# First norm, first v groups, late output projection and the samples' scores of a streaming encoder: the order of work changed

## The chip, the core and the metric

The kernel runs on one core of a Trainium2 chip. The metric is the device time of one execution in microseconds (us): the median of the runs before the change is 3111.28 us (three runs, 3106.77 to 3111.31). Engines are called PE (TensorE; its weight loads appear as PEld), DVE (VectorE), ACT (ScalarE), POOL (GpSimd) and SP (SyncE, which issues most DMAs). Two of PE's clock levels appear in the granted clock of the profile: 2.4 GHz, shown as 1.0, and 1.2 GHz, shown as 0.5.

## What is computed

One step of a 4-layer encoder with 512 tokens of a new stream (the prompt) and 8 running streams with 16 tokens each (the samples), 640 tokens in all, model width 1024:

```
for layer in range(4):                       # kinds A, B, C, A
    hp, hs = rms_norm(xp), rms_norm(xs)
    A: differential attention; prompt chunk-causal, samples over 1024 cached + 16 own positions
    B: Griffin recurrent block
    C: band attention with relative bias; samples over 512 cached + 16 own positions
    x = x + mixer(h) ;  x = x + square(relu(rms_norm(x) @ w1)) @ w2
y = rms_norm(x)

A, a sample:  p = softmax(q @ [k_cache; k_own]^T * 64**-0.5)   per head, for two half heads
              o = (p_1 - lam * p_2) @ [v_cache; v_own] ;  o = rms_norm(o) @ w_out
```

New keys and values of the attention layers and the states of layer B are outputs too.

## The kernel before, in words

**Layout.** The residual lies transposed on chip: 8 tiles `x[d]` of 128 features by 640 tokens. A matrix product in full precision is made of three matmuls with a high and a low part of each operand: high with high, low weights with high data, high weights with low data (L566 to L568 for projections to q, k and v with 256 columns; L473 to L475 with 320 columns elsewhere). ACT makes the high part (`wh` of weights, L223; `xh`, L331), DVE the low part (`wl`, L224; `xl`, L332).

**Order.** The kernel is written as loops; a scheduler then sets the order of each engine's instructions by the order in which they are emitted, a priority, and what it takes each to last. PE has eight PSUM banks under four tags: "mm" (2), "s" (2), "t" (3), "o" (1).

**First norm.** `Normed` with `first=True` makes `xh`, `xl` and squares of the eight input tiles. Squares alternate between DVE (L347) and ACT (L349); POOL adds six of them to `sacc` (L350) and DVE the last. Five matmuls with a column of ones sum over features (L375); POOL then takes the power -0.5 (L379, `rtok`), by which ACT and DVE scale the first v tiles when they leave PSUM (L581, L582).

**First v groups.** `v_group(0, tt)` for the five token tiles calls `x_group`, 24 matmuls into one bank each (tags mm, s, mm, s, t).

**Attention layers.** Eight slots (two heads of C or one head of A each); in each slot four prompt units and two sample units (q = 0, 1, four streams each) go through stages f0 to f4, and between them the projections of the next slot run. A sample unit's f0 (L785 on) makes the scores over the cache: per bank of 512 positions (two in A, one in C) four matmuls of 32 output rows side by side in the PE array (`tile_position`, L796), one for each stream. The unit's own 16 positions are four matmuls of 32 rows and 16 columns (L800) into a "t" bank. DVE takes the maximum of each piece (L816 in A, with the bias in L819 in C), ACT the exponential (L823), and POOL spreads the own block's 16 columns over a 128 x 128 tile with a 0/1 mask (L825, `eox`). f1 transposes (L838, L845), f2 multiplies with the values (L856 for the own block, L860 for the cache, 32 rows side by side again), f3 combines the halves (L877, `os` to `oc`), scales by the norm (L665 on DVE, L667 and L668 on POOL), f4 transposes `oc` (L892). For a prompt unit the same stages are L683/L684, L717, L730 (C: L741) and L751.

**Output projection.** In the last slot's steps (`s == SLOTS`) nothing is left to project, and the loop emits 21 pieces evenly over ten steps instead: one transpose, four splits (L963, L964) and 16 `early` groups, 12 matmuls each, which are the part of the output projection over the first four heads. Behind the loop come the rest of the splits and the late part.

**End.** The last MLP's output adds to `x` (L1203), ACT squares (L1210), POOL and at j = 7 DVE sum the squares (L1211), a ones matmul (L1216), the power (L1219), a broadcast (L1221), and the product to `y` (L1224), for each of the two halves of the tokens.

Of the kernel before, what the change touches and what calls it, by code (L numbers as in the profile page):

```python
# [135 lines left out]
def hybrid_encoder_kernel(ctx: ExitStack, tc: tile.TileContext, I, O):  # L136
# [165 lines left out]
    halves = load_const("halves", [P, 2])  # L302
    ropec = load_const("ropec", [P, 2, TT, 32])
# [13 lines left out]
    class Normed:  # L317
# [19 lines left out]
        def square(self, d):  # L337
            n = self.n
            self.n += 1
            if self.first:  # L340
# [4 lines left out]
                sq = self.work.tile([P, N], F32, tag="sq", name="sq", bufs=4)  # L345
# [162 lines left out]
    def attention(layer, kind, xg, aw, op):  # L508
# [50 lines left out]
        def x_group(w, tt, tag="mm"):  # L559
            acc = bank(tag)  # L560
            (h0, l0), (h1, l1) = w
            ts = slice(tt * P, (tt + 1) * P)
            for k in range(KT8):
# [7 lines left out]
        wcur = {}  # L571

        def v_group(p, tt):
# [5 lines left out]
            acc = x_group(wcur["v"], tt, ("mm", "s", "mm", "s", "t")[tt] if p == 0 else "mm")  # L579
# [202 lines left out]
        class Sample:  # L782
# [3 lines left out]
            def f0(self):  # L786
# [4 lines left out]
                sc = [bank("s") for _ in range(npc)]  # L791
                ow = bank("t")
                for c in range(npc):
                    for j in range(4):
                        b = 4 * q + j
                        pe.matmul(sc[c][32 * j:32 * j + 32, :], lhsT=z[:, b].rearrange("p a q -> p (a q)"),  # L796
                                  rhs=KV["k", s, b][:, c * 512:(c + 1) * 512], start=True, stop=True, tile_position=(0, 32 * j))
                for j in range(4):
                    b = 4 * q + j
                    pe.matmul(ow[32 * j:32 * j + 32, :16], lhsT=z[:, b].rearrange("p a q -> p (a q)"),  # L800
                              rhs=KTt[s][:, 16 * b:16 * b + 16], start=True, stop=True, tile_position=(0, 32 * j))
# [4 lines left out]
                src = [t[:, :] for t in sc] + [ow[:, :16]]  # L806
# [4 lines left out]
                eo = aw.tile([P, 16], F32, tag="eo", name="eo", bufs=2)  # L811
                self.E.append(eo)
                m = npc + 1
                for c, t in enumerate(src):
                    if is_a:
# [6 lines left out]
                for c, t in enumerate(src):  # L822
                    act.activation(self.E[c], t if is_a else self.E[c], AF.Exp, bias=st[:, 4:5], accum_out=st[:, 5 + c:6 + c])  # L823
# [587 lines left out]
    for d in range(KT8):  # L1411
        cur.add(d)
        if d >= 2:
            cur.square(d - 2)
# [196 lines left out]
```

## Time and profile before

| | us |
|---|---|
| median of three runs | 3111.28 |
| the profiled execution's own time | 3111.17 |
| its span, first to last instruction | 3109.4 |
| PE busy | 3040.6 (98%) |
| DVE busy | 2431.5 (78%) |
| ACT busy | 1619.0 (52%) |
| POOL busy | 509.7 (16%) |

The profiled execution took 0.1 us less than the median. PE is without work for some 69 us of the span. The rows are read so: a start in us from the span's first instruction, a duration, the engine, the line of the kernel, the operation, output <- input, and how many were merged (xN). In brackets behind a row stands the time that the engine was idle ahead of it and what it waited for. One fp32 matmul of the samples or of a 128 x 128 product shows as two records, a transposition as one. Matmuls overlap, so what one costs PE is the distance from its start to the next start, not its duration.

### The profile page before, as it was taken

The page shows a single profiled execution, that of the slowest core. Times are in us where ns is not written, and L with a number is a line of the kernel's source. Part 1 is how long each engine was busy: PE and PEld are TensorE (multiplying, and loading weights), DVE is VectorE, ACT ScalarE, POOL GpSimd, SP SyncE. Part 2 cuts the span into 40 slices and gives each one's busy share as a digit, 9 for nine tenths or more (in the row PEclk, how much of TensorE's full clock was granted, in tenths as well). Part 3 has the DMA queues.
Part 4 walks back from the last instruction along what each step waited for, and adds up shares of the span by engine and source line. Part 5 has one row for each costly group of instructions (what it writes and reads, how often), then busy time and mean ns, then how long its engine had stood idle before and what let it go on. Part 6 is the DMA issues. An engine that isn't in the chain of part 4 may idle for free. (4 is left out here: it accounts for less than half of the span.)

```text
span 3109.4 us, 61475 instructions
## 1 busy us (share of the span) xinstructions
PE 3040.6 (98%) x23970; PEld 2896.8 (93%) x23970; DVE 2431.5 (78%) x5197; ACT 1619.0 (52%) x3180; POOL 509.7 (16%) x676
## 2 busy tenths in 40 slices
PE   8999999999999999999999999999999999999998
PEld 7888799999999999999988889999998887999998
DVE  7777788887788788788566679788867776888877
ACT  4666554444477544445566655444446665544443
POOL 5443200000044000000222200000044432000001
PEclk9999999999999999999999999999999999999999
DMA  6877622222312322223666532222268776222223
GB/s 232 275 260 274 229 72 82 82 82 82 107 62 70 86 82 79 79 88 108 196 200 200 171 112 69 82 82 88 90 188 282 263 263 226 76 82 82 82 82 102
DMA packets 169682, 423.49 MB, mean 136 GB/s; under 512 B 19248, under 2 KB 49968, under 8 KB 169392
## 3 DMA queue, kind: packets, MB, share of 16 engines
q1 hardware_dynamic: 144336, 394.51, 37.9%
q0 software_dynamic: 4032, 9.18, 1.7%
q10 hardware_dynamic: 21024, 15.89, 1.6%
q8 instruction: 189, 3.10, 0.4%
q14 instruction: 101, 0.83, 0.1%
HBM read 379.24 MB, written 18.50 MB: 128 GB/s over the span
## 5 line engine op out<-in xcount | busy, mean ns | idle before, releaser
L223 ACT ACTIVATE wh<-raw 128x1024 fp32r<-128x1024 f32 (+1 forms) x396 | 368.8, 932 | 369.4 <-PE ps_t L1004 103.1
L224 DVE TENSOR_TENSOR wl<-raw,wh 128x1024 fp32r<-128x1024 f32 (+1 forms) x396 | 431.3, 1090 | 80.6 <-ACT wh L223 77.6
L566 PE MATMUL ps_mm<-wh,xh 128*128 128x256 f32 x1344 | 388.7, 290 | 8.4 <-ACT wh L223 8.3
L568 PE MATMUL ps_mm<-wh,xl 128*128 128x256 f32 x1344 | 387.8, 289 | 4.4 <-DVE xl L332 4.4
L567 PE MATMUL ps_mm<-wl,xh 128*128 128x256 f32 x1344 | 386.4, 288 | 0.1
L223 ACT ACTIVATE wh<-wsum 128x1024 fp32r<-128x1024 f32 x184 | 193.9, 1056 | 189.4 <-PE ps_o L1004 42.5
L566 PEld LDWEIGHTS ps_mm<-wh,xh 128*128 128x128 f32 x1344 | 256.7, 191 | 22.4 <-ACT wh L223 8.3
L568 PEld LDWEIGHTS ps_mm<-wh,xl 128*128 128x128 f32 x1344 | 256.4, 191 | 21.4 <-issue 14.8
L567 PEld LDWEIGHTS ps_mm<-wl,xh 128*128 128x128 f32 x1344 | 256.9, 191 | 8.5 <-issue 5.8
L361 POOL DMA_DIRECT2D sacc<-sq x28 | 24.9, 888 | 1295.3 <-ACT sq L359 1240.7
L224 DVE TENSOR_TENSOR wl<-wsum,wh 128x1024 fp32r<-128x1024 f32 x184 | 223.8, 1218 | 12.3 <-ACT wh L223 12.1
L1045 ACT ACTIVATE v<-v 128x640 f32<-128x640 f32 x128 | 93.2, 731 | 168.7 <-DVE v L1095 146.5
L607 POOL TENSOR_TENSOR rs<-ss,negh 128x4 f32<-128x4 f32 x120 | 130.2, 1085 | 227.0 <-DVE ss L605 182.8
L475 PE MATMUL ps_s<-hh,wl 128*128 128x320 f32 x512 | 158.3, 309 | 0.0
L475 PE MATMUL ps_mm<-hh,wl 128*128 128x320 f32 x512 | 158.2, 309 | 0.0
L474 PE MATMUL ps_mm<-hl,wh 128*128 128x320 f32 x512 | 158.2, 309 | 0.0
L473 PE MATMUL ps_mm<-hh,wh 128*128 128x320 f32 x512 | 158.2, 309 | 0.0
L473 PE MATMUL ps_s<-hh,wh 128*128 128x320 f32 x512 | 158.1, 309 | 0.0
L474 PE MATMUL ps_s<-hl,wh 128*128 128x320 f32 x512 | 158.0, 309 | 0.0
L1005 PE MATMUL ps_t<-fbh,wl 128*128 128x320 f32 x448 | 139.0, 310 | 0.0
L1003 PE MATMUL ps_t<-fbh,wh 128*128 128x320 f32 x448 | 138.8, 310 | 0.0
L1004 PE MATMUL ps_t<-fbl,wh 128*128 128x320 f32 x448 | 138.7, 310 | 0.0
(478 smaller groups left out, 10166.0 us busy)
## 6 DMA issues: line engine op xcount, KB each, us to landing
raw<-in_w SPq DMA_DIRECT2D x260, 512.0 KB, 4.1
kk<-in_cak SPq DMA_DIRECT2D x128, 512.0 KB, 6.7
vv<-in_cav SPq DMA_DIRECT2D x128, 512.0 KB, 5.8
raw<-in_wax SPq DMA_DIRECT2D x48, 512.0 KB, 4.7
kk<-in_cck SPq DMA_DIRECT2D x32, 512.0 KB, 4.6
vv<-in_ccv SPq DMA_DIRECT2D x32, 512.0 KB, 4.5
raw<-in_wcx SPq DMA_DIRECT2D x24, 512.0 KB, 4.5
sacc<-sq POOLq DMA_DIRECT2D x28, 320.0 KB, 4.6
```

The source lines that it names most:

```text
L223: act.activation(dst, src, AF.Copy)
L224: dve.tensor_sub(low, src, dst.bitcast(F32))
L473: pe.matmul(acc[:, :HALF], lhsT=wh[:, cs], rhs=a, start=k == 0, stop=False)
L474: pe.matmul(acc[:, :HALF], lhsT=wh[:, cs], rhs=b, start=False, stop=False)
L475: pe.matmul(acc[:, :HALF], lhsT=wl[:, cs], rhs=a, start=False, stop=k == ks - 1)
L566: pe.matmul(acc[:, :256], lhsT=xg.hi[k][:, ts], rhs=wh[:, cs], start=k == 0, stop=False)
L567: pe.matmul(acc[:, :256], lhsT=xg.hi[k][:, ts], rhs=wl[:, cs], start=False, stop=False)
L568: pe.matmul(acc[:, :256], lhsT=xg.lo[k][:, ts], rhs=wh[:, cs], start=False, stop=k == KT8 - 1)
L607: pool.tensor_tensor(rs, ss, negh[:, :4], op=ALU.pow)
L1003: pe.matmul(acc, lhsT=wh[:, cs], rhs=a, start=start and k == 0, stop=False, skip_group_check=True)
L1004: pe.matmul(acc, lhsT=wh[:, cs], rhs=b, start=False, stop=False, skip_group_check=True)
L1005: pe.matmul(acc, lhsT=wl[:, cs], rhs=a, start=False, stop=k == 3, skip_group_check=True)
```

## The change

Five edits, together:

- **First norm and first v groups.** All squares go to ACT, all sums to DVE; the loops first emit every `xh`/`xl` and then the squares. The five banks of the first v groups are filled feature tile by feature tile (k outermost) instead of bank after bank.
- **Own block.** The mask becomes additive (0 and -1e30). The own block is one full 128 x 128 product of four streams' queries with all 128 own keys (L810 of the changed kernel, for L800), whose other 7/8 the mask takes out; the maximum and the exponential run over 128 columns and write `eox` directly. L825 on POOL goes. In C POOL adds bias and mask into one 128 x 128 tile ahead of the maximum, and the own block's bank carries the tag "s" instead of "t".
- **Scores in one piece.** The matmuls of a unit's cache scores have a priority higher by 400 and an order among themselves (`add_manual_dep`); the two banks are taken in reverse order.
- **Late output projection.** In the last slot the 16 early groups are emitted four each in the last four steps.
- **End.** DVE sums the squares from j = 5 on.

```diff
+    dve.tensor_scalar(own, own, 1e30, -1e30, op0=ALU.mult, op1=ALU.add)
...
-                if n % 2:
-                    dve.tensor_mul(sq, x[d], x[d])
-                else:
-                    act.activation(sq, x[d], AF.Square)
-                (dve if n == KT8 - 1 else pool).tensor_add(self.acc, self.acc, sq)
+                sq = self.work.tile([P, N], F32, tag="sq", name="sq", bufs=KT8 - 1)
+                act.activation(sq, x[d], AF.Square)
+                dve.tensor_add(self.acc, self.acc, sq)
...
+                FIRST.extend(bank(t) for t in ("mm", "s", "mm", "s", "t"))
+                for k in range(KT8):
+                    for i in range(TT):
+                        x_group(wcur["v"], i, acc=FIRST[i], ks=(k,))
...
-                for j in range(4):
-                    b = 4 * q + j
-                    pe.matmul(ow[32 * j:32 * j + 32, :16], lhsT=z[:, b].rearrange("p a q -> p (a q)"),
-                              rhs=KTt[s][:, 16 * b:16 * b + 16], start=True, stop=True, tile_position=(0, 32 * j))
+                sc = [bank("s") for _ in range(npc)][::-1]
+                ow = bank("t") if is_a else bank("s")
+                with tc.high_priority(offset=400):
...
+                    for a, b in zip(g[1:], g):
+                        tc.add_manual_dep(a.ins, b.ins.name, IN_ORDER, reason="one piece")
+                pe.matmul(ow[:, :P], lhsT=z[:, 4 * q:4 * q + 4].rearrange("p b a q -> p (b a q)"), rhs=KTt[s], start=True, stop=True)
...
-                pool.tensor_mul(self.eox, eo[:, None, :].to_broadcast([P, 8, 16]),
-                                own[:, q].rearrange("p (b t) -> p b t", t=16))
+                for c in range(m):
+                    e = self.E[c] if c < npc else self.eox
+                    act.activation(e, sc[c] if is_a and c < npc else e, AF.Exp, bias=st[:, 4:5], accum_out=st[:, 5 + c:6 + c])
...
+            if s == SLOTS:
+                n = len(g) - 2 * KT8
+                tgt = [min(n, 3 * k) for k in range(nst + 1)] + [n + 4 * k for k in range(1, 5)]
...
-                    (dve if j == KT8 - 1 else pool).tensor_add(acc2, acc2, sq)
+                    (dve if j >= KT8 - 3 else pool).tensor_add(acc2, acc2, sq)
...
-        if d >= 2:
-            cur.square(d - 2)
-    cur.square(KT8 - 2)
-    cur.square(KT8 - 1)
+    for d in range(KT8):
+        cur.square(d)
```

How the change moves instructions is shown at three places. The first is DVE at the start of the program, while the x tiles are split; `sq` are squares, `sacc` their sum. Before:

```order
4 L347 TENSOR_TENSOR sq<-x_79 128x640
5 L224 TENSOR_TENSOR wl<-raw,wh 128x1024
6 L332 SCALAR_TENSOR_TENSOR xl<-x_79,gains,xh 128x640
7 L347 TENSOR_TENSOR sq<-x_83 128x640
8 L332 SCALAR_TENSOR_TENSOR xl<-x_81,gains,xh 128x640
9 L332 SCALAR_TENSOR_TENSOR xl<-x_83,gains,xh 128x640
```

After:

```order
3 L224 TENSOR_TENSOR wl<-raw,wh 128x1024 x2
4 L334 SCALAR_TENSOR_TENSOR xl<-x_79,gains,xh 128x640
5 L349 TENSOR_TENSOR sacc<-sacc,sq 128x640
6 L334 SCALAR_TENSOR_TENSOR xl<-x_81,gains,xh 128x640
7 L349 TENSOR_TENSOR sacc<-sacc,sq 128x640 x2
8 L334 SCALAR_TENSOR_TENSOR xl<-x_83,gains,xh 128x640
```

The squares have left DVE, the sums have come to it, and POOL has no row in this stretch any more. The second place is PE in the first layer, where the scores of one unit (eight matmuls `kk,qs`) and its own block (`kt,qs`) stand between projections. Before:

```order
830 L730 MATMUL ps_o<-v,et 128x128
831 L796 MATMUL ps_s<-kk,qs_235 32x512 x7
832 L717 MATMUL ps_t<-ident,e 128x128
833 L796 MATMUL ps_s<-kk,qs_235 32x512
834 L566 MATMUL ps_mm<-wh,xh 128x256
...
842 L800 MATMUL ps_t<-kt,qs_235 32x16 x4
```

After:

```order
L805 MATMUL ps_s<-kk,qs_236 32x512 x8
L889 MATMUL ps_t<-os,jq 128x128 x2
L567 MATMUL ps_mm<-wl,xh 128x256
L568 MATMUL ps_mm<-wh,xl 128x256
L566 MATMUL ps_mm<-wh,xh 128x256
L567 MATMUL ps_mm<-wl,xh 128x256
L723 MATMUL ps_t<-ident,e 128x128
L810 MATMUL ps_t<-kt,qs_236 128x128
```

The eighth score matmul stands with the other seven, and one full product stands for four tiled ones. The third place is PE at the end of the first layer's attention: the last unit's values, its halves (`os,jq`), the last transpositions and the late output projection (`oh,wh`). Before:

```order
2049 L860 MATMUL ps_o<-vv,et 32x128 x32
2050 L717 MATMUL ps_t<-ident,e 128x128 x4
2051 L751 MATMUL ps_t<-ident,oc 128x128
2052 L877 MATMUL ps_t<-os,jq 128x128
2053 L473 MATMUL ps_mm<-oh,wh 128x320
...
2065 L877 MATMUL ps_t<-os,jq 128x128
2066 L730 MATMUL ps_o<-v,et 128x128 x4
2067 L892 MATMUL ps_t<-ident,oc 128x128
2068 L751 MATMUL ps_t<-ident,oc 128x128
2069 L473 MATMUL ps_mm<-oh,wh 128x320
```

After:

```order
2070 L872 MATMUL ps_o<-vv,et 32x128 x32
2071 L723 MATMUL ps_t<-ident,e 128x128 x4
2072 L757 MATMUL ps_t<-ident,oc 128x128
2073 L889 MATMUL ps_t<-os,jq 128x128 x2
2074 L736 MATMUL ps_o<-v,et 128x128 x4
2075 L904 MATMUL ps_t<-ident,oc 128x128
2076 L757 MATMUL ps_t<-ident,oc 128x128
2077 L472 MATMUL ps_mm<-oh,wh 128x320
```

The twelve early matmuls (rows 2053 to 2064 of before) have left the tail for places further up, and both halves of the last unit's outputs stand together.

## Rows read from the trace of the kernel before

**Rows 1.** Page, first part: busy time, share and instructions of PE.
```profile
PE 3040.6 (98%) x23970; PEld 2896.8 (93%) x23970; DVE 2431.5 (78%) x5197; ACT 1619.0 (52%) x3180; POOL 509.7 (16%) x676
```

**Rows 2.** Busy time by stretch (us from:to, length, engines, clock, DMA share, GB/s).
```profile
60.00:300.00 240.00, 238.89 (x2531) 209.00 (x2530) 182.46 (x614) 150.28 (x468) 98.40 (x128) 1.00 0.78 269
386.60:393.50 6.90, 4.58 (x16) 4.00 (x16) 3.43 (x5) 3.54 (x6) 1.50 (x3) 0.51 0.22 76
```

**Rows 3.** Waits of PE, 0 to 60 us (us in total, times, longest).
```profile
PE ps_mm L566 <- ACT wh L223: 8.3, 1, 8.3
PE ps_mm L568 <- DVE xl L332: 4.4, 3, 2.5
```

**Rows 4.** Timelines of DVE, POOL and ACT at the start, and one DVE line over all.
```profile
11.81 2.19 DVE L332 SCALAR_TENSOR_TENSOR xl<-x,gains,xh 128x640 fp32r<-128x640 f32 x1
23.91 3.74 DVE L332 SCALAR_TENSOR_TENSOR xl<-x,gains,xh 128x640 fp32r<-128x640 f32 x3
10.90 4.49 POOL L350 TENSOR_TENSOR sacc<-sacc,sq 128x640 f32<-128x640 f32 x2 [10.02 <-ACT xh L331]
16.07 2.25 ACT L331 ACTIVATE xh<-x,gains 128x640 fp32r<-128x640 f32 x3
L332 DVE SCALAR_TENSOR_TENSOR xl<-x,gains,xh x32: 871/884/2187, 5.3 to 2274.6; 128x640 fp32r<-128x640 f32 x32
```

**Rows 5.** Timeline of PE around one sample unit of layer 0.
```profile
63.81 0.28 PE L567 MATMUL ps_mm<-wl,xh 128*128 128x256 f32 x1
64.02 1.92 PE L796 MATMUL ps_s<-kk,qs 128*32 128x512 f32 x16
65.88 0.39 PE L568 MATMUL ps_mm<-wh,xl 128*128 128x256 f32 x1
66.10 0.28 PE L566 MATMUL ps_mm<-wh,xh 128*128 128x256 f32 x1
66.22 0.28 PE L567 MATMUL ps_mm<-wl,xh 128*128 128x256 f32 x1
...
67.01 0.26 PE L800 MATMUL ps_t<-kt,qs 128*32 128x16 f32 x8
67.20 0.39 PE L566 MATMUL ps_mm<-wh,xh 128*128 128x256 f32 x1
...
69.81 0.38 PE L730 MATMUL ps_o<-v,et 128*128 128x128 f32 x2
...
70.15 0.28 PE L567 MATMUL ps_mm<-wl,xh 128*128 128x256 f32 x1
```

**Rows 6.** Timeline of PE where a unit's scores are broken, layer 0.
```profile
146.29 1.92 PE L796 MATMUL ps_s<-kk,qs 128*32 128x512 f32 x14
...
148.40 1.05 PE L796 MATMUL ps_s<-kk,qs 128*32 128x512 f32 x2
149.37 0.39 PE L566 MATMUL ps_mm<-wh,xh 128*128 128x256 f32 x1
```

**Rows 7.** What the score matmuls of L796 waited for, all layers (us, times).
```profile
  ACT e L690: 4.1, 6
```

**Rows 8.** Timelines at the ends of attention in layers 0 and 2: PE, then DVE.
```profile
381.49 0.39 PE L473 MATMUL ps_mm<-oh,wh 128*128 128x320 f32 x1
...
383.33 0.38 PE L877 MATMUL ps_t<-os,jq 128*128 128x128 f32 x2
...
387.58 0.47 PE L892 MATMUL ps_t<-ident,oc 128*128 128x128 f32 x1 [2.97 <-POOL oc L668]
389.87 0.64 PE L473 MATMUL ps_mm<-oh,wh 128*128 128x320 f32 x1 [1.24 <-ACT oh L963]
...
1823.11 0.49 PE L877 MATMUL ps_t<-os,jq 128*128 128x128 f32 x2 [1.23 <-DVE os L868]
...
384.47 1.22 DVE L224 TENSOR_TENSOR wl<-raw,wh 128x1024 fp32r<-128x1024 f32 x1 [0.25 <-ACT wh L223]
```

**Rows 9.** Timeline of DVE at the end of the program.
```profile
3098.34 0.49 DVE L1211 TENSOR_TENSOR fsum<-fsum,fsq 128x320 f32<-128x320 f32 x1 [1.40 <-POOL fsum L1211]
```

More of the change, by code (lines that the diff above doesn't have):

```diff
@@ L302, in hybrid_encoder_kernel @@
     halves = load_const("halves", [P, 2])
+    dve.tensor_scalar(own, own, 1e30, -1e30, op0=ALU.mult, op1=ALU.add)
+    IN_ORDER = mybir.DependencyInfo(mybir.DependencyClass.NoSync, mybir.DependencyReason.DATA)
     ropec = load_const("ropec", [P, 2, TT, 32])
@@ L557, in load_bias, with x_group @@
             SB[s] = sb
-        def x_group(w, tt, tag="mm"):
-            acc = bank(tag)
+        def x_group(w, tt, tag="mm", acc=None, ks=range(KT8)):
+            if acc is None:
+                acc = bank(tag)
             (h0, l0), (h1, l1) = w
             ts = slice(tt * P, (tt + 1) * P)
-            for k in range(KT8):
+            for k in ks:
                 wh, wl = (h0, l0) if k < 4 else (h1, l1)
@@ L569, in x_group @@
             return acc
-        wcur = {}
+        wcur, FIRST = {}, []
         def v_group(p, tt):
@@ L790, in f0 @@
                 st = aw.tile([P, 12], F32, tag="sst", name="sst", bufs=3)
-                sc = [bank("s") for _ in range(npc)]
-                ow = bank("t")
-                for c in range(npc):
-                    for j in range(4):
-                        b = 4 * q + j
[L796 to L799, printed above, removed]
-                    pe.matmul(ow[32 * j:32 * j + 32, :16], lhsT=z[:, b].rearrange("p a q -> p (a q)"),
-                              rhs=KTt[s][:, 16 * b:16 * b + 16], start=True, stop=True, tile_position=(0, 32 * j))
+                sc = [bank("s") for _ in range(npc)][::-1]
+                ow = bank("t") if is_a else bank("s")
+                with tc.high_priority(offset=400):
+                    g = []
+                    for c in range(npc):
+                        for j in range(4):
+                            b = 4 * q + j
+                            g.append(pe.matmul(sc[c][32 * j:32 * j + 32, :], lhsT=z[:, b].rearrange("p a q -> p (a q)"),
+                                               rhs=KV["k", s, b][:, c * 512:(c + 1) * 512], start=True, stop=True,
+                                               tile_position=(0, 32 * j)))
+                    for a, b in zip(g[1:], g):
+                        tc.add_manual_dep(a.ins, b.ins.name, IN_ORDER, reason="one piece")
+                pe.matmul(ow[:, :P], lhsT=z[:, 4 * q:4 * q + 4].rearrange("p b a q -> p (b a q)"), rhs=KTt[s], start=True, stop=True)
                 if q == 0:
@@ L805, in f0 @@
                     load_k(s + 1, 0)
-                src = [t[:, :] for t in sc] + [ow[:, :16]]
                 self.E = []
@@ L837, in f1 @@
                 t = bank("t")
-                pe.transpose(t[:, :P], self.eox.rearrange("p a b -> p (a b)"), ident)
+                pe.transpose(t[:, :P], self.eox, ident)
                 et = aw.tile([P, P], F32, tag="eto", name="eto", bufs=2)
```

26 lines of the change are left out of this document (14 added, 12 removed).

## The prediction

> **What bounds the kernel now.** I read the page's busy times first: PE works 3040.6 of 3109.4 us [rows 1], so PE sets the time, and it can only be shortened in two ways: less work on PE, or fewer of the 69 us in which it stands. Then the busy time by stretch: between 60 and 300 us, the heart of the first attention layer, PE is busy 238.89 of 240 us, while DVE has 182.46 and the DMA engines 0.78 of the stretch [rows 2]. So inside an attention layer a microsecond that PE does not work is a microsecond won, as long as DVE (24% free there) and the loads follow. Then PE's waits at the start: 8.3 us for the first weights, which the change does not touch, and 4.4 us in three waits for the low parts of x [rows 3]. Then the timeline of PE around a sample unit [rows 5, 6], which shows what a tiled matmul costs those around it; and last the ends of the attention layers and of the program [rows 8, 9], where PE stands for a chain over ACT, DVE and POOL. The MLPs and layer B keep their order, so these hold the same time.
>
> **First norm and first v groups.** The low part of one x tile takes DVE 0.884 us in the median and 2.187 at worst; the 2.19 at 11.81 lies beside POOL's two sums from 10.90 to 15.39 [rows 4]. All long ones lie beside POOL sums. With POOL out of this stretch, DVE has eight low parts and seven sums of about 0.8 us. ACT gets three or four more squares, some 0.7 each, like its high parts (2.25 for three [rows 4]). ACT's last high part, now ready at 18.3, comes with the squares ahead of it at about 21 (18.3 + 3.5 x 0.75); DVE, whose fifteen steps follow ACT's, has three or four of 0.8 left by then and makes the last low part at about 24, against 27.65 now (23.91 + 3.74 [rows 4]). The k-outermost order gives PE 115 matmuls that need no later tile, so PE should run without a stop from 8.3. The three waits are 4.4 us in all [rows 3]. I count 3.7 for the two long ones in full, and 1.1 for the short one with the small stops around it, room for nine matmuls of 0.12: **-4.8 us**. The rest of the chain (sum, power, v out of PSUM, first keys) moves with it. Bounds: if the loads or the DVE chain keep the longest wait of 2.5 us [rows 3], -2.3; at best -5.5, all waits and the small stops twice. One mask instruction more on DVE lies under the loads.
>
> **Own block and scores: the price of a tiled run.** In the timeline plain matmuls of 256 columns stand 0.12 apart (66.10 to 66.22). Ahead of eight score matmuls the distance is 0.21 (63.81 to 64.02), and the first plain matmul behind them takes 0.22 (65.88 to 66.10) [rows 5]. So a run of tiled matmuls costs 0.09 on the way in and 0.10 on the way out, 0.19 beside what is in it. In it: eight score matmuls 1.86 (64.02 to 65.88); four own-block matmuls 0.19 (67.01 to 67.20) [rows 5]. Scores that were broken seven and one cost 2.11 for the seven with the transposition behind them (146.29 to 148.40), no less than eight with what follows (2.08), and 0.97 more for the one (148.40 to 149.37) [rows 6]: one matmul alone costs half of what eight cost, since four lie side by side. A whole 128 x 128 product in fp32 costs 0.22 (two records of L730 and the next matmul from 69.81 to 70.15, less 0.12) [rows 5].
>
> Counting runs in the order of instructions: 160 before (55, 46 and 59 in the three attention layers), 110 after (43, 24, 43). Of 48 own blocks 37 stood alone and 11 behind scores, where I take 0.05, a quarter of 0.19, since the way in and out is paid already. Eight units had their scores broken in uneven pieces, after it one. Six more value runs are cut in halves. The sum:
> - 50 runs fewer x 0.19 = -9.5
> - seven broken pieces fewer x 0.97 = -6.8
> - tiled own blocks gone: 37 x 0.19 + 11 x 0.05 = -7.5
> - whole own blocks added: 48 x 0.22 = +10.6
> - cut value runs: no row shows one; by the switch of 0.19 they are counted above, and I add 6 x 0.15 = +0.9 inside them.
>
> Together **-12.3 us**, some -2.5 in layer 0, -6 in C, -4 in layer 3. Bounds: a switch that is partly a wait for the weights, and so not given back, leaves -12.3 + 9.5 = -2.8; the most, if a whole product cost only one of L730's two records, 0.11, is -17.6. What the change adds elsewhere lies beside PE: the maximum and the exponential over 128 columns instead of 16 on DVE and ACT (48 times, at most some 0.1 us each), for which POOL's spreading goes out of the chain exponential, mask, transposition.
>
> The Trainium skill, page "TensorEngine Tiling (Array Packing)", section "When to Use Tiling", speaks against this part: for at most 32 rows or columns it recommends four tiles side by side, which is what goes. By that rule the own block gets slower; inside a run the rows agree (0.19 against 0.22), and only the switch, which the same page names under "Key Properties" as a drain, turns it.
>
> **Late output projection.** At the end of layer 0's attention PE goes from 381.49, where the last values and transpositions are done, to the late projection at 389.87: 8.38 us, of which twelve early matmuls take 1.84 (to 383.33) and two waits 2.97 and 1.24 [rows 8]. The chain that fills it is: halves combined, copy on DVE, behind it a weight split on DVE of 1.22 us ahead of the norm's scale, POOL's power and scaling, transposition, two splits. After the change no early matmul stands in it; they are done earlier, in place of nothing, since PE is full there too. Both halves come together, and the weight split goes ahead of the copy instead of between copy and scale. From the same point I estimate 0.4 us to the combined halves, 0.3 copy, 0.45 norm, 1.5 for the scale and POOL, 2.3 from the transposition to the late projection (387.58 to 389.87): some 5.0, with 0.2 for what lies between, 5.2, against 8.38 - 1.84 = 6.54. That is -1.35 in each of layers 0 and 3 (the tail of layer 3 reads alike). In C ten early matmuls now stand where PE waits 1.23 us for the copy `os` [rows 8]: -1.2. Sum **-3.9 us**. PE's granted clock is 0.51 from 386.6 to 393.5 [rows 2], behind the wait; I leave that as it is. Bounds: +2, if the halves wait uncovered and the weight split still delays the copy (1.22 a layer [rows 8], less what was won); -7.5, if with a shorter wait the clock stays up, which gives back half of the 3.6 us from 389.87 to 393.5 in both A layers.
>
> **End.** The last sum starts at 3098.34 after 1.40 us in which DVE waited for POOL's sum [rows 9]. With DVE doing the last three sums only ACT's square of the last x, about as long as the sum's 0.49, lies between: 1.40 - 0.5 and a little, **-0.8 us**; bounds 0 and -1.2.
>
> **Sum:** -4.8 - 12.3 - 3.9 - 0.8 = -21.8 us, on the profiled execution's own 3111.17: 3089.4. That execution stands 0.1 us from the median, so I say 3089.5.
>
> **Rivals.**
> - *The switch is not given back* (other matmuls carry its wait, the weights' load or the bank it writes): part two gives -2.8 and the whole is 3111.2 - 12.3 = 3099. For it: the same 0.09 could be a stop that the next foreign kind of matmul, the whole fp32 product, meets as well (the 256-column matmul behind L730 starts its follower 0.21 later, too, which is inside my 0.22). Against it: 0.22 counted both.
> - *The whole own block is the slower one.* Its switch does not come back, since it stands beside other foreign kinds of matmul, while whole scores and merged runs gain as forecast: 37 x 0.19 = 7.0 less, 3089.4 + 7.0 = 3096.4. For it: 0.22 against 0.19 inside [rows 5]. Against it: in the same rows the matmul behind the tiled block pays. This is the result that the Trainium skill's page "TensorEngine Tiling (Array Packing)" would lead to.
> - *Slower: PSUM banks.* Scores with a raised priority take both "s" banks as soon as they can, and in C the own block wants one of them too. PE runs in order: if the bank is still read by a prompt unit's exponential, all projections behind stand. Before, the score matmuls waited 4.1 us in six waits for that exponential (L690) [rows 7], 0.7 each. If each of the 48 units waits as long once, that is 33 us: 3089.4 + 33 = 3122, slower. It decides from 0.45 us a unit. Against it: the banks' readers stand in the same distances in the order as before.
> - *The change does not do what it says*: the tails lose cover (+2 for -3.9) and only half of the start comes: 3089.4 + 5.9 + 2.5 = 3098.
>
> **How the numbers follow.** Forecast as summed, within the bounds of its parts: 0.62, 3076 to 3096. Whole own block the slower one: 0.08, about 3096. Switch not given back: 0.09; tails and start short: 0.08; both 3096 to 3105. Nothing that can be told, from parts that cancel: 0.07. Slower by the banks: 0.06, 3118 to 3140. About 0.2% (6 us) is what a measurement of this kernel can tell from no change; 3105 is that border. The range 3077 to 3104 leaves out the best end of the first case, the last two cases and the rim of the second. Faster by over 0.2%: 0.62 + 0.08 + 0.09 + 0.08 less 0.02 = 0.85; within: 0.07 + 0.02 = 0.09; slower: 0.06.
>
> **What would show it.** Start: PE without a wait between 8.3 and the ones matmul, no POOL sum, low parts at 0.88 us; the ones matmul (now L374) about 5 us earlier. Scores: eight matmuls in one row of the timeline, 0.22 around the own block, PE's busy time some 10 us shorter with about 50 switches fewer. Tails: the wait ahead of the transposition of `oc` (L904) shorter than 2.97. End: DVE's last sum within 1 us of the last x. It is wrong if PE's waits on ACT's or DVE's readers of "s" banks grow past 10 us, if PE's idle share in 60 to 300 us rises above 1%, or if the stretch from the first matmul of a layer to its last does not shrink by the sums above.

## The result and the profile after

The changed kernel takes 3091.94 us in the median of four runs (3090.58 to 3092.30); the kernel before took 3111.30 beside it. The ratio is 0.9938, with a 95% interval of 0.9924 to 0.9953: 19.4 us less. The forecast was 3089.5 with a range of 3077 to 3104. The total came out; two of its four terms did not. That the total came so close is in part luck.

The page of the changed kernel, first part, answers to [rows 1]:

```profile
span 3090.1 us, 60938 instructions
PE 3025.0 (98%) x23682; PEld 2898.4 (94%) x23682; DVE 2432.5 (79%) x5236; ACT 1624.6 (53%) x3184; POOL 477.0 (15%) x634
```

The span is 19.3 us shorter. PE's busy time fell by 15.6 us (from 3040.6), and what it stood idle fell from 68.8 to 65.1 us, by 3.7. So the gain is mostly less work on PE.

**Start.** PE's waits in the first 60 us of the changed kernel (answer to [rows 3]; us in total, times, longest):

```profile
PE ps_mm L566 <- ACT wh L223: 9.2, 1, 9.2
PE ps_mm L568 <- DVE xl L334: 0.5, 1, 0.5
```

Its DVE timeline there (answer to [rows 4]), the first low part behind the first weights and the last one:

```profile
11.59 0.88 DVE L334 SCALAR_TENSOR_TENSOR xl<-x,gains,xh 128x640 fp32r<-128x640 f32 x1
23.14 0.88 DVE L334 SCALAR_TENSOR_TENSOR xl<-x,gains,xh 128x640 fp32r<-128x640 f32 x1
```

All eight low parts take 0.88 us now, the last is ready at 24.02 (23.14 + 0.88), and 0.5 us of the 4.4 us of waits are left. In the kernel before, the three long low parts (2.15 to 2.19 us) each ended 0.7 us after the end of a sum on POOL that had begun ahead of them. PE's timeline has the ones matmul at

```profile
24.07 1.17 PE L374 MATMUL ps_t<-ones,sacc 128*128 128x1 f32 x10
```

and that of before at

```profile
29.64 1.28 PE L375 MATMUL ps_t<-ones,sacc 128*128 128x1 f32 x10
```

It moved by 5.6 us, by 6.4 if counted from each run's first matmul, since the first weights came 0.9 us later in this run (9.2 against 8.3). That arrival lies between 7.5 and 9.2 us in the traces of all kernels of this study.

**A sample unit of layer 0**, PE's timeline of the changed kernel (answer to [rows 5]):

```profile
59.83 1.92 PE L805 MATMUL ps_s<-kk,qs 128*32 128x512 f32 x16
61.68 0.39 PE L566 MATMUL ps_mm<-wh,xh 128*128 128x256 f32 x1
61.91 0.28 PE L567 MATMUL ps_mm<-wl,xh 128*128 128x256 f32 x1
62.02 0.28 PE L568 MATMUL ps_mm<-wh,xl 128*128 128x256 f32 x1
62.14 0.27 PE L723 MATMUL ps_t<-ident,e 128*128 128x128 f32 x1
62.25 0.39 PE L810 MATMUL ps_t<-kt,qs 128*128 128x128 f32 x2
62.39 0.36 PE L566 MATMUL ps_mm<-wh,xh 128*128 128x256 f32 x1
62.59 0.28 PE L567 MATMUL ps_mm<-wl,xh 128*128 128x256 f32 x1
```

Eight scores stand together. The own block costs 0.22 us: from 62.25 to 62.59 are 0.34, less 0.12 for the plain matmul in it.

**Ends of the layers**, PE's timeline at the end of layer 0's attention (answer to [rows 8]):

```profile
381.47 0.33 PE L904 MATMUL ps_t<-ident,oc 128*128 128x128 f32 x1 [1.17 <-POOL oc L674]
382.87 0.33 PE L757 MATMUL ps_t<-ident,oc 128*128 128x128 f32 x1 [1.08 <-POOL oc L674]
384.42 0.63 PE L472 MATMUL ps_mm<-oh,wh 128*128 128x320 f32 x1 [1.22 <-ACT oh L978]
```

One wait of 2.97 us became two of 1.17 and 1.08.

**By stretches.** From the starts of the first projection and of the first late projection matmul in each layer, and the first matmul of the program:

| stretch | before | after | change | forecast |
|---|---|---|---|---|
| first weights on PE | 8.31 | 9.17 | +0.9 | 0 |
| first matmul to layer 0's late projection | 381.56 | 375.25 | -6.3 | -4.8 - 2.5 - 1.35 = -8.65 |
| attention of layer 2 | 351.40 | 341.62 | -9.8 | -6 - 1.2 = -7.2 |
| from there to layer 3's first projection | 446.20 | 447.91 | +1.7 | 0 |
| attention of layer 3 | 373.05 | 367.03 | -6.0 | -4 - 1.35 = -5.35 |
| all else (MLPs, layer B, end) | | | +0.2 | -0.8 |

Each column is one execution. The kernel before and the kernel of experiment e3 have the same instructions in the same order on every engine, and yet layer 0's stretch takes 381.56 us in one and 383.62 in the other, layer 3's 373.05 and 371.99. The changed kernel and that of e9 have the same order up to the last MLP's end, and layer 2's attention takes 341.62 and 339.50. So a stretch that changes by less than some 2 us says nothing by itself.

PE's timeline at the two ends of layer 2's attention, of the kernel before:

```profile
1474.63 0.28 PE L566 MATMUL ps_mm<-wh,xh 128*128 128x256 f32 x1
...
1826.03 0.41 PE L473 MATMUL ps_mm<-oh,wh 128*128 128x320 f32 x1 [1.15 <-ACT oh L966]
```

and of the changed kernel:

```profile
1468.68 0.28 PE L566 MATMUL ps_mm<-wh,xh 128*128 128x256 f32 x1
...
1810.30 0.41 PE L472 MATMUL ps_mm<-oh,wh 128*128 128x320 f32 x1 [1.15 <-ACT oh L981]
```

### The profile page after: what moved, and what is told of

The parts are those of the page before. It is cut to its first block, busy times and chain, and to the rows that moved or that the text cites. A ratio compares the mean times of both kernels' runs of the same rounds, so it can differ in the third digit from the quotient of the medians.

```text
span 3090.1 us, 60938 instructions
## 1 busy us (share of the span) xinstructions
PE 3025.0 (98%) x23682; PEld 2898.4 (94%) x23682; DVE 2432.5 (79%) x5236; ACT 1624.6 (53%) x3184; POOL 477.0 (15%) x634
## 4 chain that ended last, share of the span: by engine, by line
PE 78%; DVE 5%; issue 2%; ACT 2%; DMA 1%; POOL 1%; SPq 0%; ACTq 0%; DVEq 0%; POOLq 0%
PE ps_t L1018 5%; PE ps_t L1020 5%; PE ps_t L1019 5%; PE ps_mm L472 4%; PE ps_mm L473 4%; PE ps_mm L474 4%; PE ps_s L472 3%; PE ps_s L473 3%; PE ps_s L474 3%; PE ps_mm L566 3%; PE ps_mm L567 3%; PE ps_mm L568 3%; PE ps_mm L1156 2%; PE ps_mm L1157 2%; PE ps_mm L1158 2%; PE ps_o L1020 2%
## 5 line engine op out<-in xcount | busy, mean ns | idle before, releaser
L224 DVE TENSOR_TENSOR wl<-wsum,wh 128x1024 fp32r<-128x1024 f32 x184 | 224.1, 1219 | 12.3 <-ACT wh L223 12.0
```

Source lines behind the costliest of these rows:

```text
L224: dve.tensor_sub(low, src, dst.bitcast(F32))
```

## The experiments

Ratios are to the kernel before on the same chip. A difference below some 3 us cannot be told by time; there the trace decides.

**Each part alone.** The first norm and v groups:

```diff
-                if n % 2:
-                    dve.tensor_mul(sq, x[d], x[d])
-                else:
-                    act.activation(sq, x[d], AF.Square)
-                (dve if n == KT8 - 1 else pool).tensor_add(self.acc, self.acc, sq)
...
+                act.activation(sq, x[d], AF.Square)
+                dve.tensor_add(self.acc, self.acc, sq)
...
+                for k in range(KT8):
+                    for i in range(TT):
+                        x_group(wcur["v"], i, acc=FIRST[i], ks=(k,))
...
```

> The kernel before with the first part alone: squares on ACT, sums on DVE, first v groups with k outermost. Theory (forecast's term): the ones matmul about 6 us earlier, PE's waits for the low parts of x gone, -4.8 us at the start. But the scheduler also sets the samples' scores in another order: still 160 tiled runs, with more broken score pieces; counted with 0.19 us a run, 0.97 us a lone score piece this costs +2.7 us. Sum -2.1 us, ratio 0.9993. Rival: broken pieces cost nothing, the start is kept whole, -4.8 us, 0.9985. Second rival: DVE's sums delay the low parts, nothing is won, 1.000.

Measured: 3106.15 us, ratio 0.9981 (0.9972 to 0.9991), -5.9 us. PE's waits at the start:

```profile
PE ps_mm L564 <- ACT wh L223: 7.8, 1, 7.8
PE ps_mm L566 <- DVE xl L332: 1.2, 2, 1.0
```

The waits for the low parts fell from 4.4 to 1.2 us. The first rival's -4.8 lies in the interval (-8.7 to -2.8 us), and the count's -2.1 just outside it. The start gave more than the 4.8 us in both of these sums, though: in the trace the 120th matmul of the v groups comes 5.5 us earlier, counted from the first. With that, less 2.7 us for broken scores, the count would be -2.8, the interval's edge. So the time shows the start and leaves the price of broken scores open. The trace has it: from the start of each score matmul to PE's next start it sums to 85.4 us in the three attention layers, against 83.0 before.

The scores' part:

```diff
-                for j in range(4):
-                    b = 4 * q + j
-                    pe.matmul(ow[32 * j:32 * j + 32, :16], lhsT=z[:, b].rearrange("p a q -> p (a q)"),
+                with tc.high_priority(offset=400):
...
+                pe.matmul(ow[:, :P], lhsT=z[:, 4 * q:4 * q + 4].rearrange("p b a q -> p (b a q)"), rhs=KTt[s], start=True, stop=True)
```

> The kernel before with whole own block, additive mask, scores in one piece and the own block's bank of C under tag s, nothing else. In the order 112 tiled runs instead of 160. Theory (a tiled run costs 0.19 us on its edges, a lone score piece 0.97, a whole product 0.22): -13.9 us, of which 9.1 are switches; with small changes at the ends of the layers -13 to -16, ratio 0.9952. Rival (the switch is not given back): -4.8 us, 0.9985. Rival (early scores hold the s banks): PE waits on readers of s banks grow by over 10 us, ratio at or above 1.

Measured: 3105.85 us, 0.9979 (0.9970 to 0.9989), -6.5 us: under half of the count. The count's -13.9 lies outside the interval (-9.3 to -3.4 us), the first rival's -4.8 inside it. So by time this run speaks for the rival that the switch is not given back. In the trace layer 2's attention is 7.0 us shorter, layer 3's 1.9, layer 0's not at all, and 3.1 us are lost again in the MLP behind layer 2. The gain lies in layer 2, then, and in the two A layers it is within what two executions differ by.

The late output projection alone:

```diff
+            if s == SLOTS:
+                n = len(g) - 2 * KT8
+                tgt = [min(n, 3 * k) for k in range(nst + 1)] + [n + 4 * k for k in range(1, 5)]
```

> The kernel before with only the new places of the early groups of the output projection in the last slot. The forecast's term for the ends of the three attention layers was -3.9 us, ratio 0.9987. Rival: the scheduler's order of every engine is the same as before, row for row, so this edit does nothing: 0 us, ratio 1.000, the same waits of 2.97 us ahead of the transposition of oc in layers 0 and 3, and what moved at the layers' ends came from the other edits.

Measured: 3110.69 us, 0.9995 (0.9985 to 1.0004), no difference. The waits of PE at the end of layer 0's attention:

```profile
PE ps_t L892 <- POOL oc L668: 3.0, 1, 3.0
PE ps_mm L474 <- DVE ol L967: 1.7, 1, 1.7
PE ps_mm L473 <- ACT oh L966: 1.2, 1, 1.2
```

The wait of 3.0 us is that of before. The interval (-4.7 to +1.2 us) would still hold the forecast's -3.9; the trace settles it: PE, DVE, ACT and POOL run the same instructions in the same order as in the kernel before, from first to last. The term of the forecast was wrong in its cause.

The end alone:

```diff
-                    (dve if j == KT8 - 1 else pool).tensor_add(acc2, acc2, sq)
+                    (dve if j >= KT8 - 3 else pool).tensor_add(acc2, acc2, sq)
```

> The kernel before with only the last three sums of squares on DVE. Forecast's term: -0.8 us. Rival, from the trace of the changed kernel, where DVE makes three x and then three sums one behind the other: between -0.6 and +0.3 us. Neither shows in the time; the distance from PE's last MLP matmul to the ones matmul tells: before 2.48 us of wait.

Measured: 3112.21 us, 0.9998 (0.9989 to 1.0007). DVE's timeline at the end of this kernel:

```profile
3092.37 3.76 DVE L1224 SCALAR_TENSOR_TENSOR y<-x,gains,ps_t 128x320 f32<-128x320 f32 x8 [1.93 <-PE ps_t L1221]
3096.84 0.48 DVE L1203 TENSOR_TENSOR x<-x,ps_s 128x320 f32<-128x320 f32 x1
3097.24 1.68 DVE L1211 TENSOR_TENSOR fsum<-fsum,fsq 128x320 f32<-128x320 f32 x3
```

PE's wait for it:

```profile
PE ps_t L1216 <- DVE fsum L1211: 2.8, 1, 2.8
```

The last sum no longer waits for POOL, but three sums now stand in a row behind three additions to x, and these behind the eight products of the first half, which start 0.65 us later than before (3092.37 against 3091.72). PE's wait grew from 2.5 to 2.8 us. The edit is worth nothing or a little less. (The changed kernel shows the same wait of 2.8 us.)

**The scores' part taken apart.** Whole own block alone, without priority and one piece:

```diff
-                for j in range(4):
-                    b = 4 * q + j
-                    pe.matmul(ow[32 * j:32 * j + 32, :16], lhsT=z[:, b].rearrange("p a q -> p (a q)"),
...
+                pe.matmul(ow[:, :P], lhsT=z[:, 4 * q:4 * q + 4].rearrange("p b a q -> p (b a q)"), rhs=KTt[s], start=True, stop=True)
...
```

> The kernel before with the whole own block and additive mask alone (own block under tag t in all layers), no raised priority, no one piece. The order then holds 134 tiled runs, not 160, but 46 units' scores stand in fours and eleven pieces are uneven. Theory by count (0.19 us a run, 0.22 a whole product, 0.97 a lone score piece): -4.9 for runs, -4.0 inside runs, +10.6 for whole products: +1.7 us, ratio 1.0005. Rival (the forecast's term of the own block: 37 runs and 48 tiled blocks go, nothing else moves): -3.9 us, 0.9987.

Measured: 3114.17 us, 1.0003 (0.9994 to 1.0013), +0.9 us. The count's +1.7 lies in the interval (-1.9 to +4.0), the rival's -3.9 does not. A cheaper operation won nothing; in the order that the scheduler then found, the scores are broken more often, and the same sum over the score matmuls is 88.2 us, against 83.0 before.

One piece alone, own block tiled:

```diff
+                with tc.high_priority(offset=400):
+                    g = []
...
+                    for a, b in zip(g[1:], g):
+                        tc.add_manual_dep(a.ins, b.ins.name, IN_ORDER, reason="one piece")
```

> The kernel before with the raised priority and the one-piece order of the scores alone, own block tiled as before. The order holds 149 tiled runs with whole pieces of eight or four. Theory by count: -10.6 us from 11 runs and 8.5 us inside runs, ratio 0.9966. Rival (early scores hold PSUM banks, so PE waits for the readers of tag s): less than half of it arrives, above 0.9985, with waits of PE on ACT and DVE of 5 us more.

Measured: 3103.03 us, 0.9971 (0.9960 to 0.9983), -9.0 us. The count's -10.6 lies in the interval (-12.4 to -5.3), the rival's -4.7 does not. This is the largest single gain.

The changed kernel with the tiled own block, its counterpart:

```diff
-                pe.matmul(ow[:, :P], lhsT=z[:, 4 * q:4 * q + 4].rearrange("p b a q -> p (b a q)"), rhs=KTt[s], start=True, stop=True)
+                for j in range(4):
+                    b = 4 * q + j
+                    pe.matmul(ow[32 * j:32 * j + 32, :16], lhsT=z[:, b].rearrange("p a q -> p (a q)"),
...
```

> The changed kernel with the own block tiled as before (0/1 mask and spreading on POOL), all else as changed. In the order 151 runs, whole pieces of scores. Theory by count against the changed kernel: +7.8 for 41 runs, +9.6 inside runs, -10.6 for whole products: +6.8 us, 3099, ratio 0.9959. Rival (the tiled form is as cheap): 3092, 0.9938.

Measured: 3097.60 us, 0.9961 (0.9947 to 0.9975). It lies between the changed kernel's 0.9938 and one piece alone, 7.2 us above the changed kernel by the ratios, as counted; the intervals of the two overlap a little. So in the changed kernel the whole own block is worth some 7 us; alone (e5) it is worth nothing. That the held scores make the difference is not shown: the scores' part alone (e2) is one piece alone (e6) with the whole own block and its other bank in C added, and at 0.9979 against 0.9971 it is no faster. It came out faster only where the start was changed too.

**The price of a tiled run by itself.** One more own block per unit, into columns that nobody reads, in the tiled form and in the whole form:

```diff
+                for j in range(4):
+                    b = 4 * q + j
+                    pe.matmul(ow[32 * j:32 * j + 32, 256:272], lhsT=z[:, b].rearrange("p a q -> p (a q)"),
...
+                pe.matmul(ow[:, 256:384], lhsT=z[:, 4 * q:4 * q + 4].rearrange("p b a q -> p (b a q)"), rhs=KTt[s], start=True, stop=True)
```

> The changed kernel with one more own block per unit, in the old tiled form (four matmuls of 32 rows, 16 columns), written beside the first into columns that nobody reads. In the order 48 of these stand alone. Theory (a tiled run pays 0.19 us at its edges): 48 x (0.19 + 0.19) = +18.1 us against the changed kernel, about 3110. Rival (no price at the edges): 48 x 0.19 = +8.9, about 3101.

> The changed kernel with one more own block per unit as a whole 128 x 128 product, written into columns that nobody reads. Theory: 48 x 0.22 = +10.6 us and the order's 111 runs, together +11.3 us against the changed kernel, about 3103, so 7 us less than the tiled one. Rival (the tiled form is the cheaper one): this run takes as long as the tiled second block or longer.

Measured: tiled 3112.44 us (1.0004, 0.9995 to 1.0013), 20 us above the changed kernel; whole 3111.39 us (1.0000, 0.9990 to 1.0009), 19 above it. The first is near the +18.1 with a price at the edges and not the rival's +8.9. The second contradicts the theory: +11.3 was expected, and by time the whole block is not told from the tiled one, as its rival said. PE's timeline of the kernel with the tiled second block:

```profile
60.91 0.39 PE L810 MATMUL ps_t<-kt,qs 128*128 128x128 f32 x2
61.22 0.26 PE L813 MATMUL ps_t<-kt,qs 128*32 128x16 f32 x8
61.41 0.39 PE L566 MATMUL ps_mm<-wh,xh 128*128 128x256 f32 x1
61.63 0.28 PE L567 MATMUL ps_mm<-wl,xh 128*128 128x256 f32 x1
```

and with the whole one:

```profile
61.17 0.39 PE L810 MATMUL ps_t<-kt,qs 128*128 128x128 f32 x2
61.40 0.39 PE L811 MATMUL ps_t<-kt,qs 128*128 128x128 f32 x2
61.54 0.36 PE L566 MATMUL ps_mm<-wh,xh 128*128 128x256 f32 x1
61.74 0.28 PE L567 MATMUL ps_mm<-wl,xh 128*128 128x256 f32 x1
```

From the first product to the second plain matmul pass 0.72 us with the tiled block and 0.57 with the whole one; without a second block it is 0.34 (62.25 to 62.59 above). So the tiled block costs 0.38 and the whole one 0.23, as forecast. These are not single cases: in 25 of the 48 units two plain matmuls of 256 columns follow, and there the distance is 0.34 us in all 25 without a second block, 0.72 in 24 of 25 with the tiled one and 0.57 in 23 of 25 with the whole one.

The times hold more than these prices. Layer 2's attention takes 354.9 us with the tiled block and 355.5 with the whole one, against 341.6 in the changed kernel, where 16 blocks are only 6.1 and 3.7 us by the prices. In both kernels PE waits there for DVE, which it does not in the changed kernel. PE's wait from 1460 to 1830 us with the tiled block:

```profile
PE ps_t L638 <- DVE ql L655: 3.5, 1, 3.5
```

and with the whole one:

```profile
PE ps_t L638 <- DVE ql L655: 5.9, 2, 3.0
```

Around that wait ten us stand by engine, clock and DMA, tiled and then whole, as

```profile
1700.00:1710.00 10.00, 7.73 (x64) 7.09 (x65) 3.99 (x16) 7.17 (x18) 0.29 (x2) 0.66 0.34 98
1700.00:1710.00 10.00, 7.40 (x72) 6.79 (x73) 4.67 (x18) 7.58 (x21) 0.29 (x2) 0.83 0.39 107
```

PE's granted clock in them is 0.66 and 0.83. So that the tiled kernel comes out near +18.1 is in part luck. Beside it the whole block is 3.4 us shorter in layer 0 and 0.8 in layer 3, but 0.6 longer in layer 2, with its second wait, and 2.1 longer between layers 0 and 2, where the edit changes nothing. The mean granted clock of the ten executions is 0.9923 with the whole block and 0.9941 with the tiled one; by an estimate, 3110 x 0.0018 = 5.6 us of a full clock. That is about what the whole block is short of the count, but no run here shows that it is the cause.

**What the two other parts do in company.** The changed kernel without the late projection's and the end's edits:

```diff
-                tgt = [min(n, 3 * k) for k in range(nst + 1)] + [n + 4 * k for k in range(1, 5)]
...
-                    (dve if j >= KT8 - 3 else pool).tensor_add(acc2, acc2, sq)
+                    (dve if j == KT8 - 1 else pool).tensor_add(acc2, acc2, sq)
```

> The changed kernel without its late output projection and without the sums on DVE at the end: start and scores together. The forecast's terms for the two (-3.9 and -0.8) would put it at 3096.6. Theory now: the first does nothing, the second at most half a microsecond, so it stands with the changed kernel at 3091 to 3094, ratio to before 0.9938, though start alone gave 0.9981 and scores alone 0.9979: what is more than their sum comes from the order that the scheduler finds for both together. Rival (the two small parts carry the missing 7 us): at or above 3098.

Measured: 3093.73 us, 0.9943 (0.9928 to 0.9958); its profiled execution, the fastest of its four, has a span of 3087.5 us. The order of its instructions is that of the changed kernel, on PE, DVE, ACT and POOL, up to the end of the last MLP, so the late projection's edit moves nothing in company either. The two edits add nothing. Start alone and scores alone sum to -12.4 us; together they give -17.7 here. Within the intervals (-2.8 to -8.7, -3.4 to -9.3, and -13.1 to -22.4) this could still be a plain sum of its best ends, but the traces lean the same way as the medians: attention of layer 2 is 7.0 us shorter in the scores-only kernel and 9.8 in the changed one, of layer 3 1.9 and 6.0. That the parts give more together is likely, then, and not shown.

The changed kernel with the first v groups emitted bank after bank:

```diff
-                for k in range(KT8):
-                    for i in range(TT):
-                        x_group(wcur["v"], i, acc=FIRST[i], ks=(k,))
...
+            acc = x_group(wcur["v"], tt, ("mm", "s", "mm", "s", "t")[tt] if p == 0 else "mm")
```

> The changed kernel with the first v groups emitted bank after bank again; first norm as changed. Theory: the scheduler interleaves the four banks by itself, the gain at the start is that of POOL's sums alone; ones matmul and the start as in the changed kernel within 0.5 us. By count the order of the scores then has 112 runs, +1.5 us: 3093, ratio 0.9942. Rival (the k-outer order makes the start): one of the waits of 1.2 and 2.5 us comes back in the first 30 us of the trace, 3095 to 3097.

Measured: 3101.94 us, 0.9969 (0.9957 to 0.9981). At the start the theory holds: the ones matmul stands 14.90 us behind the first matmul, as in the changed kernel, so the k-outer order wins nothing there. But the time is 10 us longer. In its trace layer 2's attention is 2.8 us longer and layer 3's 7.2, more than a thousand us behind the edit: the scheduler has found another order there too.

In layer 2 the clock has no part in it. The stretch (columns as in [rows 2]) in this kernel and in the changed one:

```profile
1468.40:1812.81 344.41, 341.81 (x3156) 306.94 (x3155) 214.03 (x753) 212.26 (x558) 84.12 (x117) 1.00 0.59 188
1468.68:1810.30 341.62, 338.55 (x3157) 305.77 (x3155) 216.87 (x754) 215.13 (x558) 85.38 (x117) 1.00 0.59 189
```

The granted clock is 1.00 in both, and PE stands idle no longer (2.6 and 3.1 us). What differs is a kind of tiled matmul that the count of tiled runs leaves out: the prompt's values in C, two side by side with 64 rows each. They stand in 50 runs in this kernel and in 42 in the changed one. From the start of each run to the start of what follows they take 27.9 us here and 25.9 there, 2.0 of the 2.8.

Two stretches of ten us in its layer 3:

```profile
2555.00:2565.00 10.00, 8.17 (x72) 6.38 (x68) 8.06 (x33) 6.71 (x25) 5.39 (x8) 0.83 0.96 362
2575.00:2585.00 10.00, 8.67 (x45) 7.60 (x45) 6.85 (x24) 7.20 (x20) 2.36 (x4) 0.83 0.80 261
```

and the same stretches of the changed kernel:

```profile
2555.00:2565.00 10.00, 8.57 (x107) 4.87 (x105) 9.94 (x37) 7.32 (x26) 5.32 (x6) 1.00 0.67 229
2575.00:2585.00 10.00, 10.00 (x132) 8.46 (x131) 6.81 (x24) 5.57 (x20) 0.28 (x1) 1.00 0.68 209
```

The waits ahead of the first lower clock are short ones, in its PE timeline:

```profile
2558.64 0.49 PE L730 MATMUL ps_o<-v,et 128*128 128x128 f32 x2 [0.92 <-ACT et L722]
2559.87 0.38 PE L683 MATMUL ps_s<-km,qh 128*128 128x256 f32 x1 [0.74 <-ACT e L832]
```

Of the 7.2 us of layer 3 the two stretches at 0.83 are an estimated 2 x 10 x 0.17 = 3.4, and PE's idle time is 2.1 us longer (8.2 against 6.1). The rest is left to the order: one tiled run more, and one unit's scores broken into three and five, which at 0.19 and 0.97 would be 1.2. By time too the clock is the smaller part: the two executions of this kernel with a mean clock of 0.994 and 0.995 took 3097.9 and 3098.3 us, and the changed kernel at 0.993 to 0.995 took 3090.6 to 3092.3 (the kernel before took 1.0 us less beside the latter).

The value matmuls raised like the scores, an attempt at a better kernel:

```diff
+                with tc.high_priority(offset=400):
+                    for k in range(nb):
+                        for j in range(4):
+                            pe.matmul(o[32 * j:32 * j + 32, :P], lhsT=self.ET[k // 4][:, (k % 4) * P + 32 * j:(k % 4) * P + 32 * j + 32],
...
```

> The changed kernel with the samples' value matmuls under the same raised priority as the scores, to hold them in one piece too. In the order 106 runs for 110 and fewer broken value runs. Theory by count: -2.2 us against the changed kernel, 3090, ratio 0.9931, which its interval can hardly tell from it. Rival (raised values wait for the softmax ahead of projections, PE being in order): waits of PE on ACT's et and DVE's copies grow by more than 5 us, 3097 or more.

Measured: 3106.55 us, 0.9980 (0.9971 to 0.9989): by the ratios 13 us worse than the changed kernel, as the rival said. The waits are not on the readers that the rival named. PE's longest ones in layer 3:

```profile
PE ps_s L689 <- ACT e L838: 5.1, 3, 4.2
PE ps_t L905 <- POOL oc L674: 3.0, 1, 3.0
```

A prompt unit's scores wait up to 4.2 us for ACT's exponential of a sample unit (L838), which reads the samples' scores, and the wait of 3.0 us at the layer's end is back. The mean clock is 0.992, as in the kernel with the v groups bank after bank. No kernel of the study beats the changed one beyond its interval.

## Why the prediction was right, and where it was not

- **Start, forecast -4.8: right in mechanism, a little small.** With POOL out of the stretch every low part takes 0.88 us, and the waits go but for 0.5 us. From its first matmul PE is 6.1 us ahead by the 120th matmul of the v groups, beyond the bound of -5.5; counted so, the six traces with the old first norm need 24.8 to 26.5 us and the eight with the new one 19.3 to 19.9. Part of what the term left out is the pace: the first matmuls stand 0.21 us apart instead of 0.12, 36 of them in the kernel before (until 17.95) and 27 in the changed one (until 15.51), which is 0.8 us. e1 alone gave -5.9 in time. What made it is the squares' and sums' move; the k-outer order, which the forecast named as a reason too, is not needed for it (e10).
- **Scores, forecast -12.3: the sum is near, its parts are not.** PE's busy time fell by 15.6 us, of which 2.1 lie in the start, up to the 120th matmul (20.86 to 18.76). The prices hold one by one: 0.22 to 0.23 for a whole product, 0.38 for a tiled block alone (e7, e8). What they add up to does not hold as well: with the scores' part alone the count was -13.9 and the time -6.5. (The recorded terms sum to -12.4, a tenth more.) Layer 0 gave almost nothing beyond the start (-6.3 + 6.1 = -0.2, against -3.85 with its end; two executions of one order differ by 2.1 there). Why is not settled: its runs went from 55 to 43 as counted, and no run isolates it. Layer 2 gave more than forecast (-9.8 with its end, against -7.2). There the count of 160 and 110 runs left out the prompt's values in C, which are tiled too, with 64 rows. One matmul of them (two records), in PE's timeline before:

```profile
1520.37 0.43 PE L741 MATMUL ps_o<-et,v 128*64 128x128 f32 x2
1520.73 0.39 PE L567 MATMUL ps_mm<-wl,xh 128*128 128x256 f32 x1
```

It takes 0.36 us, and runs of four and eight records take 0.37 and 0.59, so breaking these costs as well. Their runs went from 48 to 42 and their time from 27.8 to 25.9 us: 1.9 of the 2.6 us that layer 2 gave beyond the forecast.
- **Late output projection, forecast -3.9: wrong in cause.** I read the shift at the layers' ends from the order of the whole change and put it down to the edit that speaks of it. That edit moves no instruction, alone (e3) or in company (e9). The ends did change: 2.97 us of wait became 1.17 and 1.08, and C's 1.2 us ahead of `os` went; the other edits did this, through the scheduler. One piece alone (e6) has waits of 1.2 and 1.1 at the ends of both A layers, the start alone and the scores' part alone have them in layer 3 and still 3.0 in layer 0. The step that failed is the attribution, which the order with this edit alone would have shown before any run.
- **End, forecast -0.8: wrong.** The term took away a wait of DVE for POOL and did not ask what stands on DVE ahead of the new sums: eight products and three additions. PE's wait grew by 0.3 us (e4).
- **"The MLPs keep their order": wrong behind layer 2.** Its MLP takes 1.7 us more in the changed kernel (1.6 to 1.7 in e9 and e10) and 3.1 more with the scores alone. DVE's order at the start of that MLP is another one, DVE is busy without a gap there, and PE waits for it:

```profile
PE ps_s L1156 <- DVE x L1161: 1.5, 1, 1.5
PE ps_o L1020 <- DVE wl L224: 0.8, 1, 0.8
```

- **The rivals.** "The switch is not given back" falls by the timelines: e7's added run pays 0.09 on the way in and 0.10 on the way out, and e8's whole product pays neither. By time it does not fall: -4.8 fits e2. "The whole own block is the slower one" falls by the same timelines (0.23 against 0.38) and by e11 in the changed kernel, where it is 7 us; by time it is not slower alone (e5), and not told apart beside the scores (e2 and e6) or as a second block (e7 and e8). "Slower by PSUM banks" did not come: in the stretch of 60 to 300 us PE is busy 238.54 of 240 us, and its one wait of the score matmuls is 0.5 us. The price of that rival was also read too high: the 4.1 us in six waits of [rows 7] are PE's and its weight loads' together, and PE alone waited 1.7 us in three. The mechanism exists all the same: with the values raised too, one wait for a reader of such a bank was 4.2 us (e12).
- **Range.** The two terms without effect (-3.9 and -0.8), layer 0's missing gain and the losses outside the sum (+0.9 first weights, +1.7 MLP) were made up for by the ends' gains from other edits, and by a start and a layer 2 larger than forecast. That they cancel to within 2.4 us is luck. The range of 27 us was about as wide as the order's own scatter needed: e10 and the changed kernel differ by 10 us for an edit that does nothing where it stands.

The Trainium skill's page "TensorEngine Tiling (Array Packing)", "When to Use Tiling", would keep four 32-column tiles; in this kernel, where a tiled block stands alone between plain matmuls, the trace gives 0.38 us tiled and 0.23 whole. Its "Key Properties" say that changing the tiling mode drains TensorE; the rows show a price that fits it, 0.09 us in and 0.10 out.

## What to carry to other kernels

Tiled matmuls between plain ones cost 0.19 us a run at their edges here, so hold them together, or take one full product when it is only 0.22; but count runs in the order of the kernel that is built, all kinds of tiled matmul among them, since the same edit was worth nothing alone or beside the held scores, and 7 us in the full change. Before a term is put down to an edit, read the order with this edit alone: one of five edits here moved nothing. Before a stretch of a trace is explained, see what two executions of one order differ by, here up to 2 us. When an operation goes to another engine's queue, ask what stands ahead of it there, not only what it no longer waits for.

## What was not expected of the hardware

Two kernels with nearly the same work differ by 10 us (e10 and the changed one), and the granted clock is a part of it that no count has, by the estimate above 3.4 us. In e10 waits of 0.92 and 0.74 us stood ahead of ten us at a granted clock of 0.83, where the changed kernel, with waits of up to 0.68 us in the same ten us, kept 1.00. It is not the whole: layer 2 is 2.8 us longer at a clock of 1.00.

The mean clock of the profiled executions of this study lay between 0.992 and 0.996, an estimated 12 us of a full clock apart. One and the same kernel moves with it: over six executions e10 took 3097.9 us at 0.994 and 3105.1 at 0.991. So kernels whose PE work differs by a few us can come out in the other order, and times are better compared at the same mean clock.
